# Interleaving plain and mixed products in a hand-ordered transformer-layer kernel, and moving an FFN weight sum, a v store and gate loads with it

## The chip, the cores and the metric

One core of one Trainium2 chip. The metric is device time in microseconds (us) of one launch, the median of the runs taken. The core has a matrix engine (PE), three elementwise engines (DVE, ACT, POOL), a sync engine (SP) that here issues most of the DMA transfers, and 16 DMA engines behind them. Each engine works through its own list of instructions in order; semaphores tie the lists together. A DMA that has to wait for something holds up whatever stands behind it on the engine that issues it.

## The reference, cut to what matters

One encoder layer on 1024 tokens of width 1024 (float32):

```python
h = rms_norm(x, g_norm1) * (1.0 + sc1) + sh1        # sc1, sh1, ... from c @ w_ada + b_ada
proj = h @ w_in                                     # 8 heads q,k,v + 12 heads q,k,v + two gates
qa, ka, va, qb, kb, vb, gates = split(proj)
o_a = neighbourhood_attention(rms_norm(qa), rms_norm(ka), va, rpb)
o_b = dilated_window_attention(rope(rms_norm(qb)), rope(rms_norm(kb)), vb)   # three dilations, merged
gate_a, gate_b = split(sigmoid(gates + b_gate))
x = x + gt1 * ((gate_a * (o_a @ w_proj_a) + gate_b * (o_b @ w_proj_b)) @ w_o)
h2 = rms_norm(x, g_norm2) * (1.0 + sc2) + sh2
a, up = split(h2 @ w_ffn_in)
x = x + gt2 * ((silu(a) * up) @ w_ffn_out)
```

The change touches how `h @ w_in` is formed for part of the heads, and when some of the weights of later stages are loaded and summed.

## The kernel before, in words

**Number format.** Every operand of a float32 matmul is split in a high and a low part, and each product is made of three passes (`PASS`: high by high, high by low, low by high). A weight tile `raw` is turned into `whi` by an ACT copy (L129) and into `wlo` by a subtraction (L132) on POOL or DVE. The tiles come from rings with a fixed number of buffers: `raw` 6, hi and lo 10 each, and 8 larger tiles named `big` (128 partitions by 1024). A load into a ring waits until the buffer's last reader is done.

**Units, steps and chunks.** The columns of `w_in` for q, k and v form ten units of two heads or so each; a unit is 384 columns wide (256 of q and k, 128 of v). Units 1 to 3 are computed plainly. Units 4 to 9 go in three pairs, (4,5), (6,7), (8,9), which the text calls pair 0, 1 and 2. A pair is computed with 7 products instead of 8, from sums of weights and sums of tokens (a Strassen-like scheme): `p1`, `p2`, `x1`, `x2`, `x4`, `x3`, `w22` in this order. A product is 4 tiles of 128 tokens (t0 to t3) by 4 chunks along the inner dimension; one chunk is three matmuls, L1183. So a pair is 112 chunks. The chunks of all units stand in one list, `stream`; the main loop runs over steps n = 6 to 91, and each takes the next 7 chunks (10 before step 28, 8 before step 10) and puts the attention work of earlier units between them. Pair 0 begins at chunk 192 (step 27), pair 1 at 304, pair 2 at 416; they end near step 75. Steps 76 to 91 compute the gates (`gate_pre`, matmul L832), again by sums of tokens and weights.

**What a product needs.** Products `p1`, `p2` and `x4` read plain tokens, which lie in SBUF (`hT`). Products `x1`, `x2`, `x3` and `w22` read mixed tokens (sums of tokens made earlier and kept in DRAM as `t_d`); SP loads them tile by tile, in a high and a low part (`sload`, L1169) into buffers of the hi and lo rings, named `smix`, every third one into a spare part of `hT`. When a product starts at chunk s, `sload` of tile t is issued at chunk s+4t-8, and the tile is needed at chunk s+4t. Its weights are loaded at s-27, -24, -21, -18 (L120, and L1140 for the tile `chain` of `x1`), mixed on POOL from s-17 on (L1145 to L1151) and split from s-14 on. `when(chunk, f)` hangs such work on a chunk.

**Where a product goes.** Each tile's result sits in one of two PSUM buffers `ps_d`, and the next but one tile waits for that buffer. `pair_evac` empties it: `p1` is copied to a sum A by ACT (L1116); `x1` makes B = A + p (L1118, DVE); `p2` finishes a tile of the pair's first unit out of A; `x2` adds to A and B (L1120, L1121); `x4`, `x3` and `w22` finish tiles out of B, B and A. A and B are slices of spare `hT` space. Finishing is `proj_post`: DVE adds the q and k part of the sum and PSUM into `qn` (L369); DVE adds the v part into a tile `vs` (L407), which ACT's DMA queue stores to `v_d` (L412); then come the norm (L372 to L387, ACT and DVE) and the rotation on POOL (L394 to L397). `vs` has two buffers, so the third add waits until the first store has landed.

**Other work in the same steps.** `w1_combos` (L900 to L917) forms sums of four tiles of a first FFN weight and keeps them in DRAM for later. It runs twice, in five parts on five consecutive steps: part 0 has SP load four tiles of 256 KB into two `big` buffers (L905), parts 1 to 4 are one POOL operation each (L909 to L915), and part 4 stores the four results. `W1MIX` sets the first step: 30 and 47. The adaLN modulation is computed along the way (weights `wa`, DVE multiply-adds L340, transposes L301). For the gates, `mixed_load` at step 76 loads 2 MB of mixed tokens (L777), and `gate_prep` by the table `GPREP` loads and splits gate weights: for the first pair of gates, part 0 at step 74 loads and splits the weights of the first two products, part 1 at step 77 loads the rest (L120 and L816), sums them (L820, L822 on POOL) and splits them.

**What sets the order.** PE's order is the order of the program, by hand. On the other engines a scheduler orders by priority and expected times, except for pinned work (most DMAs on SP, the POOL sums), which keeps program order.

Of the kernel before, what the change touches and what calls it, by code (L numbers as in the profile page):

```python
# [10 lines left out]
F32 = mybir.dt.float32  # L11
# [37 lines left out]
def hybrid_layer(ctx: ExitStack, tc: tile.TileContext, x, colp, wada1, wada2, bada2, wqkv, wg, wpa, wpb,  # L49
# [121 lines left out]
    ap_ = pool("attn", "right")  # L171
# [10 lines left out]
    yT = [ap_.tile([128, 4, S], F32, tag="qk", bufs=2, name="yT") for _ in range(2)]  # L182
    land = [big("land") for _ in range(NLAND)]
    for tag, n, bufs in (("bm", 512, 1), ("p", 512, 4), ("qn", 256, 9), ("rtab", 512, 1), ("acc2", 512, 1), ("pT", 512, 4),
                         ("stg", 512, 2), ("vs", 128, 2), ("ra", 64, 2), ("rb", 64, 2)):
        ap_.tile([128, n], F32, tag=tag, bufs=bufs, name="place")
    seq = [0]

# [45 lines left out]
            nc.vector.tensor_tensor_reduce(junk, xts[t], xts[t], 1.0, 0.0, ALU.mult, ALU.add, acc)  # L234

    def x_rstd(p):
        v, y, z = (ap_.tile([128, 2], F32, tag=f"xs{i}", bufs=2, name=f"xs{i}") for i in range(3))
        nc.scalar.activation(y, ss2[p], AF.Ln, scale=1.0 / D, bias=eps)
        nc.vector.tensor_scalar(v, ss2[p], 1.0 / D, EPS, op0=ALU.mult, op1=ALU.add)
        nc.scalar.activation(y, y, AF.Exp, scale=-0.5)  # L240
        nc.vector.tensor_mul(z, y, v)
        nc.vector.scalar_tensor_tensor(z, z, -0.5, y, op0=ALU.mult, op1=ALU.mult)
        nc.vector.scalar_tensor_tensor(y, z, 1.5, y, op0=ALU.add, op1=ALU.mult)
        xr[p] = y
# [115 lines left out]
        return deco  # L360

    @urgent(PP)
    def proj_post(U, t, pd=None, acc=None):
        pd = U.pd[t] if pd is None else pd
        qn = ap_.tile([128, 4, 64], F32, tag="qn", bufs=9, name="qn")
        U.qn[t] = qn
        pq = pd[:, :256].rearrange("p (h d) -> p h d", h=4)
        if acc is not None:
            nc.vector.tensor_add(qn, acc[:, :256].rearrange("p (h d) -> p h d", h=4), pq)  # L369
        vs = v_out(U, t, pd, acc)  # L370
        sq = ap_.tile([128, 256], F32, tag="sq", bufs=1, name="sq")
        nc.scalar.activation(sq, pd[:, :256] if acc is None else qn.rearrange("p h d -> p (h d)"), AF.Square)  # L372
        if acc is None:
            nc.scalar.activation(qn, pq, AF.Copy, scale=-1.0 / 128)
# [5 lines left out]
        nc.scalar.activation(y2, y, AF.Square)  # L380
        nc.vector.scalar_tensor_tensor(z, ss, 64 * EPS, y2, op0=ALU.add, op1=ALU.mult)
        nc.vector.scalar_tensor_tensor(r, z, -192.0, y, op0=ALU.add, op1=ALU.mult)
        rr = r[:, :, None].to_broadcast([128, 4, 64])
        if acc is None:
            nc.vector.tensor_tensor(qn, qn, rr, op=ALU.mult)
        else:
            nc.vector.scalar_tensor_tensor(qn, qn, -1.0 / 128, rr, op0=ALU.mult, op1=ALU.mult)  # L387
        if U.kind < 3:
            ra = ap_.tile([128, 4, 16], F32, tag="ra", bufs=2, name="ra")
            rb = ap_.tile([128, 4, 16], F32, tag="rb", bufs=2, name="rb")  # L390
            tb = U.tab[:, t]
            v4 = lambda z: z.rearrange("p (a b) c -> p a b c", a=2)
            tv = lambda f, c0, c1: tb[:, f, :, None, c0:c1].to_broadcast([128, 2, 2, c1 - c0])
            nc.gpsimd.tensor_tensor(v4(ra), v4(qn[:, :, 0:16]), tv(0, 0, 16), op=ALU.mult)  # L394
            nc.gpsimd.tensor_tensor(v4(rb[:, :, 0:8]), v4(qn[:, :, 8:16]), tv(1, 0, 8), op=ALU.mult)
            nc.gpsimd.tensor_tensor(v4(rb[:, :, 8:16]), v4(qn[:, :, 0:8]), tv(1, 8, 16), op=ALU.mult)
            nc.gpsimd.tensor_tensor(qn[:, :, 0:16], ra, rb, op=ALU.add)  # L397

    def v_out(U, t, pd, acc):
        if U.kind == 0:  # L400
            nc.scalar.activation(U.v[:, t, :], pd[:, 256:384], AF.Copy)
            return
        vs = ap_.tile([128, 128], F32, tag="vs", bufs=2, name="vs")
        if acc is None:
            nc.scalar.activation(vs, pd[:, 256:384], AF.Copy)
        else:
            nc.vector.tensor_add(vs, acc[:, 256:384], pd[:, 256:384])  # L407
# [382 lines left out]
    def gate_raw(i, q):  # L790
        return wload(wg[i, :, 4 * q:4 * q + 4, :], 512, True)
# [7 lines left out]

    def gate_prep(p, part):  # L800
        pr = GPAIRS[p]
        if part == 0:
            for i in pr if p == 0 else ():
                for q in (0, 1):
                    graw[i, q] = gate_raw(i, q)
            for nm, q in (("w11", 0), ("w12", 1)):
                for i in pr:
                    gwt[i, nm] = wsplit(graw[i, q])
            return
        if p == 0:  # L810
            z = big("wgx")
            for i in pr:
                for q in (2, 3):
                    graw[i, q] = gate_raw(i, q) if i == pr[0] else z[:, 512 * q - 1024:512 * q - 512]
            for q in (2, 3):
                pin(nc.sync.dma_start(graw[pr[1], q], wg[pr[1], :, 4 * q:4 * q + 4, :]))  # L816
        eng = nc.vector if p == 3 else nc.gpsimd
        for i in pr:
            r = [graw.pop((i, q)) for q in range(4)]
            eng.tensor_add(r[2], r[2], r[3])  # L820
# [102 lines left out]
    U = new_unit(0, w0)  # L923
# [141 lines left out]
    def when(p, f):  # L1065
        events.setdefault(p, []).append(f)

    def unit_of(u, w=None):
        if u == len(units):
            units.append(new_unit(u, w))  # L1070
        return units[u]
# [23 lines left out]
            for k in range(KT):  # L1095
                stream.append(lambda t=t, k=k: job(t, k))

    PROD = ("p1", "p2", "x1", "x2", "x4", "x3", "w22")
    SRC = {"p1": (0, 0), "p2": (0, 4), "x1": (1, 4), "x2": (0, 0), "x4": (0, 4), "x3": (1, 4), "w22": (1, 4)}
    sums, nmix = [], [0]  # L1100

    def pair_evac(nm, t, pd, ua, ub):
        if not sums:
            sums.extend(spare(q, 1536, F32) for q in range(2))
        A, B = (z[:, 384 * t:384 * t + 384] for z in sums)
        p = pd[:, :384]
        if nm == "p2":
            proj_post(unit_of(ua), t, pd, A)
        elif nm == "x4":
            proj_post(unit_of(ua), 4 + t, pd, B)  # L1110
        elif nm == "w22":
            proj_post(unit_of(ub), t, pd, A)
        else:
            with tc.high_priority(PP):
                if nm == "p1":
                    nc.scalar.activation(A, p, AF.Copy)  # L1116
                elif nm == "x1":
                    nc.vector.tensor_add(B, A, p)  # L1118
                elif nm == "x2":
                    nc.vector.tensor_add(A, A, p)  # L1120
                    nc.vector.tensor_add(B, B, p)  # L1121
                else:
                    nc.vector.tensor_add(A, A, p)
            if nm == "x3":
                proj_post(unit_of(ub), 4 + t, pd, B)

    def pair_units(ua):
        ub = ua + 1
        chain, ch = [], {}
        for nm in PROD:  # L1130
            s = len(stream)
            r, w = {}, {}
            e, k0 = SRC[nm]
            for k in range(4):
# [24 lines left out]
            for t in range(4):  # L1159
                sm = {}  # L1160
                if nm in TD:
# [7 lines left out]
                            pin(nc.sync.dma_start(fview(z).rearrange("p (k q) -> p k q", k=4), t_d[q, TD[nm], t]))  # L1169
# [790 lines left out]
```

## Time and profile before

| what | value |
|---|---|
| median of 3 runs | 1509.71 us (1507.7 to 1511.85) |
| profiled execution | 1507.33 us |
| its span, first to last instruction | 1505.5 us |
| granted PE clock, mean | 0.991 |
| PE busy | 1461.3 us, 97% of the span |
| PE weight load busy | 1240.9 us |
| DVE, ACT, POOL busy | 1096.3, 711.2, 732.5 us |
| DMA | 285.17 MB, 189 GB/s mean |

How to read it: a profile row gives the time of an instruction from the span's start, its duration, engine, source line and tiles ("out<-in"). In brackets stands how long the engine had been idle before it and what ended that idle time. A matmul's record is longer than the distance between two matmuls, because they are pipelined: a record of 128x384 reads some 0.33 us, and the next one starts some 0.16 us later.

### The profile page before, as it was taken

How to read it: one execution, taken by the hardware profiler on the slowest of the kernel's cores; microseconds unless marked ns; L12 is line 12 of the kernel's file. 1: busy time of each engine (PE TensorE's matmuls, PEld its weight loads, DVE VectorE, ACT ScalarE, POOL GpSimd, SP SyncE). 2: the span in 40 equal slices, each digit the busy share in tenths (PEclk: the TensorE clock that was granted, in tenths of full speed). 3: DMA queues.
4: the chain of work that ended last, by engine and by line, in shares of the span. 5: the costliest groups of instructions: out<-in, count | busy, mean ns of one | idle time of the engine just before them, and what ended most of it. 6: DMA issues, size and time to landing. Idle time of an engine off the chain costs nothing.

```text
span 1505.5 us, 24463 instructions
## 1 busy us (share of the span) xinstructions
PE 1461.3 (97%) x8024; PEld 1240.9 (82%) x8024; DVE 1096.3 (73%) x2144; ACT 711.2 (47%) x1807; POOL 732.5 (49%) x706
## 2 busy tenths in 40 slices
PE   8999998988999999999999999999999999999998
PEld 7999987888788777888888888888888888887886
DVE  6788856867877865576774597788767777599468
ACT  5666654654677865355432354233223333354442
POOL 0452357557354257247432301677767776104464
PEclk9999999999999999999999999999999999999999
DMA  9657769759855575693452225345443334898343
GB/s 355 235 176 238 206 196 305 229 177 297 260 178 175 175 242 198 229 351 99 130 203 96 90 89 181 126 130 179 151 129 107 110 106 145 277 374 281 98 151 102
DMA packets 189264, 285.17 MB, mean 189 GB/s; under 512 B 29488, under 2 KB 91600, under 8 KB 188368
## 3 DMA queue, kind: packets, MB, share of 16 engines
q1 hardware_dynamic: 170560, 269.96, 54.0%
q10 hardware_dynamic: 18576, 13.64, 2.8%
q8 instruction: 64, 1.05, 0.3%
q14 instruction: 64, 0.52, 0.1%
HBM read 218.67 MB, written 64.86 MB: 188 GB/s over the span
## 4 chain that ended last, share of the span: by engine, by line
PE 81%; DVE 7%; DMA 7%; ACT 2%; issue 2%; SPq 1%; POOL 0%; ACTq 0%; DVEq 0%; POOLq 0%
PE ps_v L1625 7%; PE ps_d L1625 7%; PE ps_s L1625 7%; PE ps_d L1183 7%; PE ps_t L1625 6%; PE ps_d L351 6%; PE ps_d L832 5%; PE ps_s L1795 3%; PE ps_d L1795 3%; PE ps_s L1560 2%; PE ps_d L1560 2%; PE ps_v L1795 2%; PE ps_t L1795 2%; PE ps_v L1560 1%; PE ps_v L832 1%
## 5 line engine op out<-in xcount | busy, mean ns | idle before, releaser
L129 ACT ACTIVATE whi<-raw 128x512 fp32r<-128x512 f32 (+2 forms) x313 | 182.0, 594 | 209.3 <-PE ps_s L1795 38.0
L132 POOL TENSOR_TENSOR wlo<-raw,whi 128x512 fp32r<-128x512 f32 (+2 forms) x142 | 178.9, 1268 | 176.7 <-ACT whi L129 161.1
L132 DVE TENSOR_TENSOR wlo<-raw,whi 128x512 fp32r<-128x512 f32 (+1 forms) x171 | 152.0, 906 | 55.2 <-ACT whi L129 50.0
L1183 PE MATMUL ps_d<-whi,hT 128*128 128x384 f32 x416 | 120.1, 353 | 17.1 <-DVE vs L407 5.3
L351 PE MATMUL ps_d<-whi,hT 128*128 128x384 f32 x384 | 101.2, 338 | 0.0
L1575 POOL TENSOR_TENSOR e<-e,c 128x512 f32<-128x512 f32 x44 | 68.8, 1565 | 61.1 <-DVE c L1705 37.0
L1183 PEld LDWEIGHTS ps_d<-whi,hT 128*128 128x128 f32 x416 | 78.9, 195 | 20.9 <-issue 7.1
L129 ACT ACTIVATE whi<-ws 128x512 fp32r<-128x512 f32 x60 | 37.7, 628 | 119.4 <-DVE ws L1642 76.8
L832 PE MATMUL ps_d<-hT,whi 128*128 128x512 f32 x256 | 81.8, 401 | 0.1
L1183 PE MATMUL ps_d<-whi,smix 128*128 128x384 f32 x256 | 73.8, 348 | 7.7 <-DMA smix<-t_d 5.1
L132 POOL TENSOR_TENSOR wlo<-m,whi 128x512 fp32r<-128x512 f32 x35 | 51.3, 1476 | 55.0 <-ACT whi L129 55.0
L1573 ACT ACTIVATE e<-e 128x512 f32<-128x512 f32 x44 | 27.5, 631 | 93.8 <-DVE e L1708 64.7
L1183 PE MATMUL ps_d<-wlo,hT 128*128 128x384 f32 x208 | 71.7, 345 | 0.0
L351 PEld LDWEIGHTS ps_d<-whi,hT 128*128 128x128 f32 x384 | 69.6, 188 | 0.6 <-issue 0.6
L132 POOL TENSOR_TENSOR wlo<-chain,whi 128x384 fp32r<-128x384 f32 x36 | 38.0, 1057 | 55.4 <-ACT whi L129 53.6
L351 PE MATMUL ps_d<-wlo,hT 128*128 128x384 f32 x192 | 64.2, 334 | 0.0
L619 ACT ACTIVATE P<-P,st 128x256 f32<-128x256 f32 (+2 forms) x100 | 45.7, 458 | 28.8 <-DVE st L617 28.5
L1625 PE MATMUL ps_v<-h2T,whi 128*128 128x512 f32 x192 | 59.2, 389 | 0.0
L1625 PE MATMUL ps_s<-h2T,whi 128*128 128x512 f32 x192 | 59.1, 389 | 0.0
L340 DVE SCALAR_TENSOR_TENSOR acc<-wa,cact,acc 128x512 f32<-128x512 f32 x56 | 50.2, 897 | 10.7 <-DMA wa<-in_wada_dram 10.5
L1625 PE MATMUL ps_d<-h2T,whi 128*128 128x512 f32 x184 | 56.7, 390 | 0.0
L1574 DVE TENSOR_TENSOR e<-e 128x512 f32<-128x512 f32 x44 | 43.7, 1000 | 17.2 <-ACT e L1573 17.0
(447 smaller groups left out, 4498.6 us busy)
## 6 DMA issues: line engine op xcount, KB each, us to landing
raw<-in_w_dram SPq DMA_DIRECT2D x139, 256.0 KB, 3.1
raw<-in_wqkv_dram SPq DMA_DIRECT2D x116, 192.0 KB, 4.2
ga_d<-e SPq DMA_DIRECT2D x77, 256.0 KB, 2.0
raw<-ga_d SPq DMA_DIRECT2D x77, 256.0 KB, 2.7
wa<-in_wada_dram SPq DMA_DIRECT2D x32, 512.0 KB, 5.4
smix<-t_d SPq DMA_DIRECT2D x64, 256.0 KB, 3.0
m<-in_w_dram SPq DMA_DIRECT2D x44, 256.0 KB, 5.3
hT<-t_d SPq DMA_DIRECT2D x40, 256.0 KB, 5.1
```

Of the source, the lines that this page charges most:

```text
L129: h = nc.scalar.activation(hi[:, :n], r, AF.Copy)
L132: (eng or nc.gpsimd).tensor_sub(lo[:, :n], r, fview(hi[:, :n]))
L340: nc.vector.scalar_tensor_tensor(ada_acc[c], wa, cact[:, kk:kk + 1], ada_acc[c], op0=ALU.mult, op1=ALU.add)
L351: nc.tensor.matmul(pd[:, :384], tok(a, k, t), U.w[k][b][:, :384], start=(k == 0 and i == 0), stop=(k == KT - 1 and i == 2))
L619: nc.scalar.activation(C.P[h][:nq, c], C.P[h][:nq, c], AF.Exp, scale=-1.0, bias=nm, accum_out=sm)
L832: nc.tensor.matmul(pb, w[x][:, k * 128:(k + 1) * 128], b[y][k], start=(k == 0 and q == 0), stop=(k == 3 and q == 2))
L1183: nc.tensor.matmul(pd[:, :384], lhs, w[k][b][:, :384], start=(k == 0 and i == 0), stop=(k == 3 and i == 2))
L1560: nc.tensor.matmul(pbs[hf], h2T[a][:, k, t * 128:(t + 1) * 128], wow[hf, k][b], start=(n == 0 and (a, b) == PASS[0]), stop=(n == KT - 1 an ...
L1574: nc.vector.tensor_mul(sg, sg, a)
L1575: nc.gpsimd.tensor_mul(sg, sg, up)
L1625: nc.tensor.matmul(pb, w[p][:, k * 128:(k + 1) * 128], b[q][:, k], start=(k == 0 and i == 0), stop=(k == 3 and i == 2))
L1795: nc.tensor.matmul(pb[m], o[0][a][:, m * 128:(m + 1) * 128], o[1][b], start=(k == 0 and i == 0), stop=(k == HT - 1 and i == 2))
```

## The change

1. **Order of products.** In each pair the order is now `p1`, `x1`, `p2`, `x2`, `x4`, `x3`, `w22`: plain and mixed tokens alternate at the start of the pair. The weights and tokens of `x1` are thereby needed 16 chunks earlier, those of `p2` 16 later.
2. **FFN weight sums.** `W1MIX` is (69, 74) instead of (30, 47).
3. **Token loads.** For `x1`, `x2` and `x3` the tiles t0, t1, t2 are issued at s-15+3t instead of s+4t-8: 7, 8 and 9 chunks earlier. t3 and all of `w22` stay.
4. **v.** `vs` gets three buffers. In the products of the pair's second unit (`x3`, `w22`) the v part is not summed into `vs` but in place into the sum tile (B or A), and the store to `v_d` reads that.
5. **Gate loads.** For the first pair of gates the loads of part 0 are at step 73 (split at 74 as before), those of part 1 at step 75 (sums and splits at 77 as before).
6. The splits of the very first product (`p1` of pair 0) are no longer pinned.
7. Small tiles: `x_rstd` shares buffers of the tags rv, ry, rz, and a filler `AFILL` shrinks from 384 to 64, which makes room for the third `vs`.

From about line 800 on, lines of the changed kernel lie three higher: L1183 becomes L1186, L905 becomes L908.

```diff
-GPREP = {74: (0, 0), 77: (0, 1), 82: (1, 0), ...}
-W1MIX = (30, 47)
+GPREP = {73: (0, -2), 74: (0, 0), 75: (0, -1), 77: (0, 1), 82: (1, 0), ...}
+W1MIX = (69, 74)
...
-                         ("stg", 512, 2), ("vs", 128, 2), ("ra", 64, 2), ("rb", 64, 2)):
+                         ("stg", 512, 2), ("vs", 128, 3), ("ra", 64, 2), ("rb", 64, 2)):
...
-    def v_out(U, t, pd, acc):
+    def v_out(U, t, pd, acc, here):
...
-        vs = ap_.tile([128, 128], F32, tag="vs", bufs=2, name="vs")
+        vs = acc[:, 256:384] if here else ap_.tile([128, 128], F32, tag="vs", bufs=3, name="vs")
...
     def gate_prep(p, part):
         pr = GPAIRS[p]
-        if part == 0:
-            for i in pr if p == 0 else ():
+        if part == -2:
+            for i in pr:
                 for q in (0, 1):
                     graw[i, q] = gate_raw(i, q)
+            return
+        if part == 0:
             for nm, q in (("w11", 0), ("w12", 1)):
                 for i in pr:
                     gwt[i, nm] = wsplit(graw[i, q])
             return
-        if p == 0:
+        if part == -1:
             z = big("wgx")
...
+            return
         eng = nc.vector if p == 3 else nc.gpsimd
...
-    PROD = ("p1", "p2", "x1", "x2", "x4", "x3", "w22")
+    PROD = ("p1", "x1", "p2", "x2", "x4", "x3", "w22")
...
         elif nm == "w22":
-            proj_post(unit_of(ub), t, pd, A)
+            proj_post(unit_of(ub), t, pd, A, True)
...
             if nm == "x3":
-                proj_post(unit_of(ub), 4 + t, pd, B)
+                proj_post(unit_of(ub), 4 + t, pd, B, True)
...
-                    w[k] = wsplit(ch[k] if nm in ("x1", "x2", "x3") else r[k], None, True)
+                    w[k] = wsplit(ch[k] if nm in ("x1", "x2", "x3") else r[k], None, s > 192)
...
-                    when(s + 4 * t - 8, sload)
+                    when(s - 15 + 3 * t if nm in ("x1", "x2", "x3") and t < 3 else s + 4 * t - 8, sload)
```

How the change moves instructions stands in the prediction, at the places it speaks of; there the rows name an engine's instructions in program order, by line and tile.

More of the change, by code (lines that the diff above doesn't have):

```diff
@@ L30 @@
 GPHASE = ("w11", "w12", "x1", "x4")
-GPREP = {74: (0, 0), 77: (0, 1), 82: (1, 0), 84: (1, 1), 86: (2, 0), 88: (2, 1), 90: (3, 0)}
+GPREP = {73: (0, -2), 74: (0, 0), 75: (0, -1), 77: (0, 1), 82: (1, 0), 84: (1, 1), 86: (2, 0), 88: (2, 1), 90: (3, 0)}
 GLOAD = {81: 1, 85: 2, 89: 3}
-W1MIX = (30, 47)
+W1MIX = (69, 74)
 MC11 = {0: (5, 6, 7, 2), 1: (0, 1)}
@@ L39 @@
 PP, QT, AQ, AT, AV = 100, 0, 0, 0, 0
-EDGE, CFILL, AFILL, OFILL = 480, 64, 384, 32
+EDGE, CFILL, AFILL, OFILL = 480, 64, 64, 32
 WARM = 40
@@ L236, in x_rstd @@
     def x_rstd(p):
-        v, y, z = (ap_.tile([128, 2], F32, tag=f"xs{i}", bufs=2, name=f"xs{i}") for i in range(3))
+        v, y, z = (ap_.tile([128, 2], F32, tag=i, bufs=3, name="xs") for i in ("rv", "ry", "rz"))
         nc.scalar.activation(y, ss2[p], AF.Ln, scale=1.0 / D, bias=eps)
@@ L362, in proj_post @@
     @urgent(PP)
-    def proj_post(U, t, pd=None, acc=None):
+    def proj_post(U, t, pd=None, acc=None, here=False):
         pd = U.pd[t] if pd is None else pd
@@ L369, in proj_post @@
             nc.vector.tensor_add(qn, acc[:, :256].rearrange("p (h d) -> p h d", h=4), pq)
-        vs = v_out(U, t, pd, acc)
+        v_out(U, t, pd, acc, here)
         sq = ap_.tile([128, 256], F32, tag="sq", bufs=1, name="sq")
```

## The prediction

> **What bounds the kernel now.** I read the page first: PE is busy nearly all of the span, and the chain that ended last lies on PE for the most part, with DVE and DMA behind it.
>
> ```profile
> PE 1461.3 (97%) x8024; PEld 1240.9 (82%) x8024; DVE 1096.3 (73%) x2144; ACT 711.2 (47%) x1807; POOL 732.5 (49%) x706
> PE 81%; DVE 7%; DMA 7%; ACT 2%; issue 2%; SPq 1%; POOL 0%; ACTq 0%; DVEq 0%; POOLq 0%
> ```
>
> The change removes no matmul, so it can only fill idle time of PE. The second view is a table by stretches (columns: stretch, its length, busy time of PE, PE weight load, DVE, ACT and POOL, granted clock, DMA share, GB/s).
>
> ```profile
> 560.00:1350.00 790.00, 790.00 (x3628) 652.32 (x3627) 568.80 (x778) 302.40 (x562) 400.60 (x282) 1.00 0.49 166
> 240.00:250.00 10.00, 9.71 (x68) 8.94 (x69) 7.76 (x18) 4.75 (x15) 9.54 (x9) 0.83 1.07 396
> 300.00:310.00 10.00, 4.91 (x36) 4.23 (x37) 9.40 (x26) 4.45 (x19) 5.88 (x11) 0.75 0.76 245
> 310.00:320.00 10.00, 10.00 (x62) 9.42 (x60) 2.73 (x11) 6.30 (x21) 7.87 (x14) 0.91 0.70 227
> 350.00:360.00 10.00, 6.55 (x35) 5.58 (x36) 7.48 (x8) 2.10 (x4) 10.00 (x9) 0.83 1.08 374
> 420.00:430.00 10.00, 7.71 (x57) 6.72 (x56) 7.34 (x25) 7.44 (x25) 3.93 (x5) 1.00 0.47 142
> 440.00:470.00 30.00, 30.00 (x226) 26.79 (x225) 20.33 (x64) 20.14 (x63) 17.55 (x18) 1.00 0.72 230
> 530.00:540.00 10.00, 7.75 (x45) 5.50 (x44) 4.97 (x14) 5.59 (x16) 7.46 (x6) 0.86 0.61 223
> ```
>
> From 560 to 1350 us PE never idles. The idle time that can be had lies in the pairs and the first gates, 200 to 540 us. There the clock falls after a long gap: 0.75 in the stretch of the longest one. So a gap costs its length and, behind it, (1 - clock) times the stretch. The third view is PE's timeline around its large gaps (start, duration, what; in brackets the gap and what ended it).
>
> ```profile
> 205.13 0.44 PE L1183 MATMUL ps_d<-whi,hT 128*128 128x384 f32 x1 [2.79 <-ACT qn L374]
> 233.12 0.41 PE L1183 MATMUL ps_d<-whi,smix 128*128 128x384 f32 x1 [1.53 <-DVE hT L1118]
> 234.67 0.62 PE L1183 MATMUL ps_d<-whi,smix 128*128 128x384 f32 x2 [0.96 <-DMA smix<-t_d]
> 240.29 0.66 PE L1183 MATMUL ps_d<-whi,hT 128*128 128x384 f32 x1 [3.61 <-DMA hT<-t_d]
> 295.48 0.41 PE L1183 MATMUL ps_d<-whi,hT 128*128 128x384 f32 x1 [1.68 <-DMA hT<-t_d]
> 305.25 0.66 PE L1183 MATMUL ps_d<-whi,hT 128*128 128x384 f32 x1 [5.09 <-DVE vs L407]
> 354.81 0.41 PE L1183 MATMUL ps_d<-whi,smix 128*128 128x384 f32 x1 [3.45 <-DMA smix<-t_d]
> 386.45 0.43 PE L301 MATMUL ps_t<-acc,ones 128*32 128x128 f32 x8 [2.15 <-ACT PT L641]
> 399.75 0.41 PE L1183 MATMUL ps_d<-whi,smix 128*128 128x384 f32 x1 [1.08 <-DVE vs L407]
> 425.30 0.44 PE L1183 MATMUL ps_d<-whi,hT 128*128 128x384 f32 x1 [2.29 <-ACT hT L1116]
> 535.50 0.50 PE L832 MATMUL ps_d<-hT,wlo 128*128 128x512 f32 x1 [2.17 <-POOL wlo L132]
> ```
>
> These eleven gaps add to 26.8 us. I take them one by one: is the wait that ended last still there after the change?
>
> **The change part by part.**
>
> *FFN weight sums away from steps 30 and 47, tokens of x1 earlier (term 1).* The gaps at 233 to 240 us are in x1 of pair 0, t1 and t2. SP's timeline shows why its tokens were late, and the table of waits of SP what held it:
>
> ```profile
> 214.08 13.31 SPq L905 DMA_DIRECT2D w1m<-in_w_dram x4
> 227.49 0.38 SPq L120 DMA_DIRECT2D raw<-in_wqkv_dram x1
> 227.97 3.63 SPq L1169 DMA_DIRECT2D smix<-t_d x2
> ...
> SPq L905 <- DMA v_d<-vs: 16.6, 3, 6.8
> SPq L1169 <- PE ps_d L1183: 43.6, 24, 5.6
> ```
>
> The four loads of w1m held SP for 13.31 us, and the tokens queued behind. In program order, SP at this place reads before (x1's t0 is row 100, t1 row 104):
>
> ```order
> 98 L1140 DMA chain<-in_wqkv_dram 128x384
> 99 L120 DMA raw<-in_wqkv_dram 128x384 x2
> 100 L1169 DMA smix<-t_d 128x512 x2
> 101 L120 DMA raw<-in_wqkv_dram 128x384
> 102 L905 DMA w1m<-in_w_dram 128x512 x4
> 103 L120 DMA raw<-in_wqkv_dram 128x384
> 104 L1169 DMA smix<-t_d 128x512 x2
> ```
>
> and now, for the same tiles of x1 (t0 row 97, t1 row 102, t2 row 104):
>
> ```order
> 97 L1172 DMA smix<-t_d 128x512 x2
> 98 L325 DMA brow<-in_bada_dram 128x1x128
> 99 L315 DMA wa_3176<-in_wada_dram 128x1024
> 100 L315 DMA wa_3317<-in_wada_dram 128x1024
> 101 L315 DMA wa_3466<-in_wada_dram 128x1024
> 102 L1172 DMA smix<-t_d 128x512 x2
> 103 L120 DMA raw<-in_wqkv_dram 128x384
> 104 L1172 DMA hT<-t_d 128x512 x2
> ```
>
> The w1m loads are gone from between the tokens; adaLN weights stand there instead. The row of the pair's matmuls gives the time of a chunk:
>
> ```profile
> L1183 PE MATMUL ps_d<-whi,hT x416: 333/334/660, 200.1 to 508.7; 128*128 128x384 f32 x139
> ```
>
> 308.6 us over 336 chunks of the three pairs is 0.92 us. t1 and t2 are now issued 16 and 17 chunks, about 15 us, before use, where it was 8 chunks, 7.3 us. Gone: 1.53 + 0.96 + 3.61 = 6.10, and (1 - 0.83) x 10 = 1.7 of clock behind them: **-7.8**.
>
> *Token of x2 in pair 1 (term 2).* The gap of 3.45 at 354.81 waited for a token that is now asked for 8 chunks, 7.4 us, earlier: more than it was late. With 1.7 of clock (350 to 360): **-5.1**.
>
> *v in place (term 3).* The longest gap, 5.09, is the first tile of pair 1, which waits for the PSUM buffer of pair 0's last product. DVE's and ACT's timelines before it:
>
> ```profile
> 298.24 0.41 DVE L369 TENSOR_TENSOR qn<-hT,ps_d 128x256 f32<-128x256 f32 x1
> 300.11 0.16 DVE L381 SCALAR_TENSOR_TENSOR rz<-ss,ry 128x4 f32<-128x4 f32 x1 [1.46 <-ACT ry L380]
> 301.73 1.55 DVE L340 SCALAR_TENSOR_TENSOR acc<-wa,cact,acc 128x512 f32<-128x512 f32 x1
> 304.82 0.28 DVE L407 TENSOR_TENSOR vs<-hT,ps_d 128x128 f32<-128x128 f32 x1
> 299.87 0.21 ACT L380 ACTIVATE ry<-rv 128x4 f32<-128x4 f32 x1 [1.91 <-DMA u_d<-stg]
> ```
>
> L369 has read its part of the buffer at 298.65; L407, which frees it, starts at 304.82. With two vs tiles the scheduler had put seven instructions between, among them L381, which waits for an ACT instruction behind a store's issue. The DVE program from L369 of this tile (t2 of w22) to its L407, before:
>
> ```order
> 585 L369 TENSOR_TENSOR qn<-hT,ps_d 128x256
> 586 L381 SCALAR_TENSOR_TENSOR rz<-ss_4518,ry 128x4
> 587 L340 SCALAR_TENSOR_TENSOR acc_4330<-wa_4554,cact,acc_4330 128x512
> 588 L382 SCALAR_TENSOR_TENSOR rz<-rz,rv 128x4
> 589 L340 SCALAR_TENSOR_TENSOR acc_4330<-wa_4554,cact,acc_4330 128x512
> 590 L387 SCALAR_TENSOR_TENSOR qn<-qn,rz 128x256
> 591 L376 TENSOR_REDUCE ss_4620<-sq 128x4
> 592 L381 SCALAR_TENSOR_TENSOR rz<-ss_4574,ry 128x4
> 593 L407 TENSOR_TENSOR vs<-hT,ps_d 128x128
> ```
>
> and now, from t1's L369 to t2's L407:
>
> ```order
> 578 L369 TENSOR_TENSOR qn<-hT,ps_d 128x256
> 579 L407 TENSOR_TENSOR hT<-hT,ps_d 128x128
> 580 L376 TENSOR_REDUCE ss_4556<-sq 128x4
> 581 L381 SCALAR_TENSOR_TENSOR rz<-ss_4499,ry 128x4
> 582 L382 SCALAR_TENSOR_TENSOR rz<-rz,rv 128x4
> 583 L369 TENSOR_TENSOR qn<-hT,ps_d 128x256
> 584 L407 TENSOR_TENSOR hT<-hT,ps_d 128x128
> ```
>
> L407 follows L369 directly and waits for no store. The buffer is free some 6 us sooner, so all 5.09 go. Behind it the clock costs (1 - 0.75) x 10 + (1 - 0.91) x 10 = 3.4, less 0.1 that falls into the gap: **-8.4**. The gap at 399.75, also L407: **-1.1**.
>
> *Gate loads (term 4).* The gap at 535.50 waits for a low part that POOL made late, since the weights came late. SP's and POOL's timelines:
>
> ```profile
> 518.48 5.84 SPq L777 DMA_DIRECT2D hT<-t_d x8
> 525.14 0.92 SPq L120 DMA_DIRECT2D raw<-in_wg_dram x2
> 530.58 1.29 POOL L820 TENSOR_TENSOR raw<-raw 128x512 f32<-128x512 f32 x1 [20.52 <-DMA raw<-in_wg_dram]
> ```
>
> The weights stood behind 2 MB of mixed tokens. In SP's program they now stand ahead of them (before):
>
> ```order
> 246 L867 DMA sig_d<-ga 128x512
> 247 L777 DMA hT<-t_d 128x4x128 x8
> 248 L867 DMA sig_d<-ga 128x512
> 249 L120 DMA raw<-in_wg_dram 128x512 x2
> 250 L816 DMA wgx<-in_wg_dram 128x512 x2
> ```
>
> and now:
>
> ```order
> 247 L920 DMA w_d<-w1m 128x512 x4
> 248 L120 DMA raw<-in_wg_dram 128x512 x4
> 249 L908 DMA w1m<-in_w_dram 128x512 x4
> 250 L120 DMA raw<-in_wg_dram 128x512 x2
> 251 L818 DMA wgx<-in_wg_dram 128x512 x2
> 252 L870 DMA sig_d<-ga 128x512
> 253 L777 DMA hT<-t_d 128x4x128 x8
> ```
>
> The loads pass 9 transfers, the first of which waited for the gate result. POOL had been idle for 20.52 us, so its sums start as soon as the loads land, at the latest the 6.66 us earlier that lie between 518.48 and 525.14. Gone: 2.17, and (1 - 0.86) x 10 = 1.4 of clock: **-3.6**. Here a rule bears on it: the Trainium skill (TensorE: Matmul & The Clock Gate, "What's actually happening") says that the clock halves after about 3.4 us of idle time, in windows that run free. By that rule alone this gap of 2.17 would cost no clock and the forecast would be 1.4 us higher. The trace shows it both ways: 0.86 behind 2.17 here, 1.00 behind 2.29 in the stretch from 420; I go by the trace.
>
> *What stays.* The gaps at 205.13 (ACT late), 295.48 (w22 keeps its load step), 386.45 and 425.30 (ACT in order) have no cause that the change removes: 0, between -8.9 (their sum, should the new order dissolve them) and 0.
>
> *What is added.* The w1m loads, sums and stores now fall at steps 69 to 78, about 470 to 520 us. One POOL sum, and the room there:
>
> ```profile
> L909 POOL TENSOR_TENSOR w1m<-w1m x2: 1260/1272/1283, 236.5 to 346.9; 128x512 f32<-128x512 f32 x2
> 480.00:500.00 20.00, 20.00 (x152) 18.10 (x151) 18.37 (x66) 17.13 (x61) 4.28 (x4) 1.00 0.65 198
> 510.00:520.00 10.00, 8.63 (x60) 5.77 (x59) 7.81 (x33) 8.70 (x30) 0.06 (x1) 1.00 0.19 51
> ```
>
> Four sums of 1.27 us, 5.1 a set, meet a POOL that is busy for 4.28 of 20 and 0.06 of 10 us; DMA is at 0.19 in the second stretch. I take 0. If the loads block SP for 13.31 us again, the last w22's tokens lose their cover of 8 chunks, 7.3 us: 13.31 - 7.3 = 6 us at most.
>
> x1 needs its weights 16 chunks earlier in pair 0, right at the start of the pair. A sum there and a split take about 1 us each on POOL:
>
> ```profile
> L1145 POOL TENSOR_TENSOR chain<-chain,raw x12: 1000/1008/1021, 211.7 to 429.2; 128x384 f32<-128x384 f32 x12
> ```
>
> Four of each are 8 us, within the 14.7 us of the product p1, but not much ahead of it. If each of four inner chunks comes one such operation late, that is 4 us; if none, 0. I take 2. Last, reshuffled work on ACT and DVE can meet PE anew: between 0 and one gap of the size of 425.30 a pair, 6.9; I take one, 2.3.
>
> Sum: -7.8 - 5.1 - 8.4 - 1.1 - 3.6 + 2 + 2.3 = -21.7. The profiled execution took 1507.33, so 1485.6; it lies 2.4 below the median of 1509.71, and on that footing the forecast is **1488**. Its own range: -26 with half of the four others gone (-4.5) gives 1479; with costs of 4 and 6.9, 1494.6.
>
> **The rivals.** 0.3%, about what a measurement can tell here, is 4.5 us.
>
> *Tokens stay late, 0.2.* SP's waits for buffers that PE frees are 43.6 us in 24 waits before; a load that is issued earlier only waits longer if its buffer's reader sets the time. Then term 2 and half of term 1 stay: -21.7 + 5.1 + 3.9 = -12.7, **1497**. For it: that row. Against it: the waits that ended the gaps are transfers behind other transfers, and 3.45 is less than what is gained.
>
> *Earlier tokens block SP, slower, 0.07.* The loads of x1, x2 and x3 stand 7 to 9 chunks earlier on SP, ahead of weight loads. If they wait for buffers there, the weights behind them come late. Weights have 13 chunks, 12 us, from load to split; the longest wait for a buffer was 5.6, so two such in a row, with a slow landing, decide it. At the price of term 2, 5.1 a product, nine products cost 46: 1488 + 46 = **1534**; from six products on it is slower. The Trainium skill (DMA: Bandwidth & Descriptors, "Anatomy of one DMA") says that a semaphore wait is served by the issuing sequencer before dispatch, so whatever is behind waits too. The 13.31 us of SP above agree.
>
> *Other waits take over, 0.1.* If pairs are bound by DVE and ACT throughout, and not by single waits, what is freed is lost at the next buffer: **1507**, within 0.3%. For it: DVE is busy for 9.40 of 10 us before the longest gap. Against it: from 440 to 470 the same products ran with PE at 30.00 of 30 and DVE at 20.33.
>
> **How the numbers follow.** Forecast 0.6, rivals 0.2, 0.07 and 0.1, 0.03 for the rest. Faster: 0.6 + 0.2 and a part of the rest, 0.82; same 0.1; slower 0.08. The range runs from 1478 (under the forecast's low end) over the first rival with its costs at the upper bounds, 1497 + 6.6 = 1504; it leaves out 0.2.
>
> **What would show it.** Right: no gap over 1 us that ends on L407, or on a token of x1 or x2; the stretch around 305 us of the pair boundary at clock 1.00; the first gate products after pair 2 without a gap; gaps left at the first p1 and around adaLN's transposes. Wrong: SP's w1m loads holding it for over 7 us near 470 or 505; POOL's wlo ending PE's gaps in x1 of pair 0; SP's waits for PE's buffers well over 43.6 with weight splits late.

## The result and the profile after

| | before | changed |
|---|---|---|
| median | 1508.7 us (4 runs, 1504.68 to 1511.85) | 1494.12 us (4 runs, 1493.69 to 1495.56) |
| profiled execution, its span | 1507.33, 1505.5 us | 1495.56, 1493.8 us |

The ratio is 0.9906, with a 95% interval of 0.9881 to 0.9932: faster by 0.9%, some 14 us. The forecast was a gain of 21.7 us, with a range that holds the measured time.

The page of the changed kernel: the work is the same, PE is busy 3 us less, and the span is 11.7 shorter.

```profile
PE 1458.3 (98%) x8024; PEld 1237.0 (83%) x8024; DVE 1102.1 (74%) x2144; ACT 711.0 (48%) x1807; POOL 732.3 (49%) x706
```

From 200 to 560 us the kernel before had 14 gaps of PE of 0.5 us and more, 28.7 us in all; the changed kernel has 20, 22.7 us in all. Nine of the 20, from PE's timeline (start, duration, what; in brackets the gap and what ended it):

```profile
204.26 0.45 PE L1186 MATMUL ps_d<-whi,hT 128*128 128x384 f32 x1 [1.48 <-ACT qn L374]
239.93 0.41 PE L1186 MATMUL ps_d<-whi,smix 128*128 128x384 f32 x1 [1.42 <-DVE vs L407]
302.72 0.45 PE L1186 MATMUL ps_d<-whi,hT 128*128 128x384 f32 x1 [2.39 <-ACT hT L1119]
351.95 0.44 PE L1186 MATMUL ps_d<-whi,hT 128*128 128x384 f32 x1 [1.86 <-DVE hT L1124]
383.10 0.41 PE L1186 MATMUL ps_d<-whi,smix 128*128 128x384 f32 x1 [1.16 <-DVE rz L382]
384.47 0.64 PE L1186 MATMUL ps_d<-whi,smix 128*128 128x384 f32 x2 [0.78 <-DMA smix<-t_d]
498.73 0.73 PE L835 MATMUL ps_d<-hT,whi 128*128 128x512 f32 x2 [0.97 <-ACT whi L129]
500.08 0.50 PE L835 MATMUL ps_d<-hT,wlo 128*128 128x512 f32 x1 [0.63 <-POOL wlo L132]
503.57 0.70 PE L581 MATMUL ps_v<-PT,v 128*64 128x128 f32 x4 [0.91 <-ACT PT L572]
```

None of the gaps of 3.4 to 5.1 us is left; the longest is 2.39. But PE's waits from 200 to 560 us (what for: us in total, times, longest) show how many smaller ones took their place:

```profile
PE ps_d L1186 <- ACT hT L1119: 3.5, 3, 2.4
PE ps_d L1186 <- DVE hT L1124: 2.8, 2, 1.9
PE ps_d L1186 <- DVE vs L407: 2.3, 2, 1.4
PE ps_v L438 <- DVE tot L705: 1.7, 1, 1.7
PE ps_d L1186 <- DMA smix<-t_d: 0.8, 1, 0.8
```

Tokens (smix) are down to 0.8 us. What ends most of the waits now is DVE and ACT; the first three rows, 8.6 us, are instructions that empty PSUM. The stretches, with the granted clock third from the end:

```profile
300.00:310.00 10.00, 7.61 (x53) 6.97 (x54) 3.16 (x10) 4.71 (x15) 7.54 (x12) 0.83 0.87 305
380.00:390.00 10.00, 8.06 (x40) 6.79 (x39) 7.24 (x24) 5.60 (x22) 2.99 (x3) 0.83 1.02 263
500.00:510.00 10.00, 9.01 (x40) 6.66 (x40) 7.93 (x22) 9.05 (x29) 9.67 (x9) 0.66 0.54 167
550.00:1340.00 790.00, 790.00 (x3628) 652.51 (x3627) 569.35 (x777) 301.18 (x560) 400.76 (x281) 1.00 0.49 166
```

By (1 - clock) times the stretch, an estimate that also counts idle time within a stretch, the clock costs 1.7 + 1.7 + 3.4 = 6.8 us there. In the kernel before it cost 1.7 + 3.4 + 1.7 + 1.4 = 8.2 in the stretches shown with the prediction, and 3.2 in two more:

```profile
200.00:210.00 10.00, 7.21 (x33) 6.89 (x32) 4.50 (x18) 7.04 (x24) 4.28 (x10) 0.83 0.74 227
380.00:390.00 10.00, 7.85 (x57) 7.01 (x56) 7.97 (x24) 6.10 (x19) 3.44 (x3) 0.85 0.78 236
```

So by this estimate 11.4 - 6.8 = 4.6 of the 11.7 us of span are clock. The pages of the two profiles give less: PE's busy time, for the same 8024 matmuls, fell by 3.0 us, and the other 8.7 us are idle time. The stretch without gaps behind (550 to 1340) is as long as before.

### The profile page after: what moved, and what is told of

The parts are those of the page before. It is cut to its first block, busy times and chain, and to the rows that moved or that the text cites. A ratio compares the mean times of both kernels' runs of the same rounds, so it can differ in the third digit from the quotient of the medians.

```text
span 1493.8 us, 24484 instructions
## 1 busy us (share of the span) xinstructions
PE 1458.3 (98%) x8024; PEld 1237.0 (83%) x8024; DVE 1102.1 (74%) x2144; ACT 711.0 (48%) x1807; POOL 732.3 (49%) x706
## 4 chain that ended last, share of the span: by engine, by line
PE 61%; DVE 4%; issue 1%; DMA 1%; ACT 1%; POOL 0%; SPq 0%; ACTq 0%; DVEq 0%; POOLq 0%
PE ps_v L1628 7%; PE ps_d L1628 7%; PE ps_s L1628 7%; PE ps_t L1628 6%; PE ps_d L835 6%; PE ps_s L1798 3%; PE ps_d L1798 2%; PE ps_d L1563 2%; PE ps_s L1563 2%; PE ps_t L1798 2%; PE ps_v L1798 2%; DVE wlo L132 1%; PE ps_v L1563 1%; PE ps_v L835 1%; PE ps_v L1414 1%; PE ps_t L1414 1%
## 5 line engine op out<-in xcount | busy, mean ns | idle before, releaser
L1186 PE MATMUL ps_d<-whi,hT 128*128 128x384 f32 x416 | 118.3, 347 | 9.8 <-DVE hT L1124 2.8
L1186 PEld LDWEIGHTS ps_d<-whi,hT 128*128 128x128 f32 x416 | 77.0, 190 | 14.6 <-PE ps_d L1186 4.4
L1186 PE MATMUL ps_d<-whi,smix 128*128 128x384 f32 x256 | 73.8, 346 | 6.5 <-DVE vs L407 1.4
L1186 PE MATMUL ps_d<-wlo,hT 128*128 128x384 f32 x208 | 70.6, 339 | 1.0 <-POOL wlo L132 1.0
L132 POOL TENSOR_TENSOR wlo<-gl,whi 128x512 fp32r<-128x512 f32 x30 | 40.1, 1352 | 34.3 <-ACT whi L129 34.3
L394 POOL TENSOR_TENSOR ra<-qn,rtab 128x64 f32<-128x64 f32 x48 | 21.0, 437 | 71.3 <-DVE qn L385 50.0
```

Source lines behind the costliest of these rows:

```text
L132: (eng or nc.gpsimd).tensor_sub(lo[:, :n], r, fview(hi[:, :n]))
L1186: nc.tensor.matmul(pd[:, :384], lhs, w[k][b][:, :384], start=(k == 0 and i == 0), stop=(k == 3 and i == 2))
```

## The experiments

All times are set against the kernel before on the same chip; "loss" is a kernel's ratio less the changed kernel's 0.9906, times 1509 us, and each ratio is known to about 0.2%, 3 us. My theory was that each part of the change removes its own gaps (terms). The rivals: the parts stand in for each other or need each other; or freed time is lost at the next wait.

Where a kernel gains or loses is seen by the first matmul of each pair and of the gates, counted off in the traces (336 records of L1183 or L1186 a pair). The times are us from the span's start, from one profiled execution of each kernel; executions of one kernel differ by some us.

| first matmul of | before | changed | u_w1 | u_sload | u_order | u_gate | u_v2 |
|---|---|---|---|---|---|---|---|
| pair 0 | 200.1 | 200.5 | 200.7 | 199.5 | 199.9 | 200.5 | 200.3 |
| pair 1 | 305.3 | 292.3 | 298.3 | 297.1 | 296.9 | 292.9 | 296.7 |
| pair 2 | 405.7 | 390.8 | 405.6 | 399.9 | 402.9 | 389.5 | 394.1 |
| gates | 508.9 | 498.7 | 508.7 | 508.7 | 511.3 | 500.3 | 500.1 |
| end of the span | 1505.5 | 1493.8 | 1500.1 | 1503.9 | 1506.0 | 1506.8 | 1494.8 |

The changed kernel gains 14.9 us up to the start of pair 2, and loses 4.7 of them again between there and the first gate product.

### FFN weight sums put back: u_w1

```diff
-W1MIX = (69, 74)
+W1MIX = (30, 47)
```

> The changed kernel with the FFN weight sums back at steps 30 and 47. Theory of terms (each part of the change removes its own gaps): the 7.8 us of the gaps in x1 of pair 0 come back, so about 6 to 8 us slower than the changed kernel's 1494.1. Theory of cover (the early token loads alone already hide SP's block of 13.31 us, and the sums cost something at their new place, where the gate products now wait 0.97 + 0.63 + 0.91 us and the clock is 0.66 from 500 to 510 us): at most 2 us slower, or up to 4 us faster, and the stretch 500 to 510 back at clock 1.00.

Measured: 0.9946 (0.9925 to 0.9967), a loss of 6.0 us. That is near the size of the term, but not its mechanism. No wait of x1 in pair 0 came back. The 6 us are also a balance: by the table u_w1 is 14.8 us behind the changed kernel at the start of pair 2, and only 6.3 at the end. From 500 to 510 us its clock is 1.00, and its first gate products do not wait, as the theory of cover had it for this stretch; so the sums cost something at their new place. In pair 0 PE waits at x4 for a low part, and POOL's timeline shows why:

```profile
258.68 0.69 PE L1186 MATMUL ps_d<-wlo,hT 128*128 128x384 f32 x1 [2.35 <-POOL wlo L132]
255.46 1.27 POOL L918 TENSOR_TENSOR w1m<-w1m 128x512 f32<-128x512 f32 x1
256.69 0.98 POOL L1152 TENSOR_TENSOR raw<-raw,chain 128x384 f32<-128x384 f32 x1
257.64 1.94 POOL L132 TENSOR_TENSOR wlo<-raw,whi 128x384 fp32r<-128x384 f32 x2
214.07 3.50 SPq L908 DMA_DIRECT2D w1m<-in_w_dram x4
```

A sum of the FFN weights (L918, 1.27 us) stands on POOL between x4's own sums and splits. This wait is one of several that are longer than in the changed kernel (2.87 at the first tile of x2 in pair 0 for 1.42, 2.69 at the first tile of x4 in pair 1 for 0.92); what makes the others longer was not traced. On SP the four loads now hold the queue for 3.50 us where it was 13.31 in the kernel before, with the tokens already ahead of them.

### Token loads put back: u_sload

```diff
-when(s - 15 + 3 * t if nm in ("x1", "x2", "x3") and t < 3 else s + 4 * t - 8, sload)
+when(s + 4 * t - 8, sload)
```

> The changed kernel with the token loads of x1, x2, x3 back at s+4t-8. Theory of terms: term 2, the token of x2 in pair 1, comes back, 5.1 us, and perhaps part of x1's gaps: 5 to 8 us slower than 1494.1. Theory of cover (without the w1m loads in the way the old lead of 8 chunks is enough): within 2 us of 1494.1, no gap over 1 us that ends on a token.

Measured: 0.9971 (0.9954 to 0.9987), a loss of 9.8 us, more than either theory said, and again for the most part not through tokens: PE's waits on them are 4.4 us from 200 to 560, where they are 0.8 in the changed kernel, and 2.08 of them are in w22, whose loads are the same in both. The largest gap is at the first tile of x2 in pair 1. PE's and DVE's timelines:

```profile
345.25 0.66 PE L1186 MATMUL ps_d<-whi,hT 128*128 128x384 f32 x1 [5.45 <-ACT sq L372]
335.70 1.50 DVE L340 SCALAR_TENSOR_TENSOR acc<-wa,cact,acc 128x512 f32<-128x512 f32 x1 [1.37 <-DMA wa<-in_wada_dram]
337.45 1.18 DVE L340 SCALAR_TENSOR_TENSOR acc<-wa,cact,acc 128x512 f32<-128x512 f32 x1
339.45 0.74 DVE L340 SCALAR_TENSOR_TENSOR acc<-wa,cact,acc 128x512 f32<-128x512 f32 x1
340.98 1.56 DVE L340 SCALAR_TENSOR_TENSOR acc<-wa,cact,acc 128x512 f32<-128x512 f32 x1
344.32 0.41 DVE L369 TENSOR_TENSOR qn<-hT,ps_d 128x256 f32<-128x256 f32 x1
```

What empties the PSUM buffer of p2 (L369, and L407 behind it at 344.72) stands on DVE behind four adaLN operations, the first of which waited for its weights `wa`. The profile names ACT as what ended PE's wait, but L407 on DVE is what frees the buffer. In the changed kernel the L369 of the same tile (t2 of p2) runs ten us sooner, ahead of the adaLN operations, 0.3 us after the tile's last matmul where it is 6.6 in u_sload:

```profile
334.04 0.41 DVE L369 TENSOR_TENSOR qn<-hT,ps_d 128x256 f32<-128x256 f32 x1
342.56 2.44 DVE L340 SCALAR_TENSOR_TENSOR acc<-wa,cact,acc 128x512 f32<-128x512 f32 x2
```

Loads of `wa` and tokens share SP; with the tokens moved, the adaLN work stands elsewhere relative to p2. How the scheduler came to this order no run shows.

### Both put back: u_w1_sload

> Both of the above undone. Theory of terms: 7.8 + 5.1 = 13 us slower, so about 1507, with gaps that end on tokens of x1 or x2. Theory of cover: each part alone hid the same gaps, so only both together bring them back: more than the sum of the two single kernels' losses. Rival (other waits take over): less than 5 us slower.

Measured: 1.0041 (1.0026 to 1.0057), slower than the kernel before, a loss of 20.4 us where the single losses add to 15.8. The excess of 4.6 us is on the side of the theory of cover, but within the joint uncertainty of four ratios (some 6 us), so it is not shown that the parts stand in for each other. The gaps that came back are not those on tokens of x1 that the theory meant: PE's largest are 6.84 and 4.59, at the first tile of x2 in pairs 1 and 0, where p2's sums on DVE come late. What is left of the change, the new order above all, is a loss without these two parts.

### The order alone, and all but the order: b_order, u_order

In b_order only the line of `PROD` differs from the kernel before; in u_order only that line differs from the changed kernel.

> The changed kernel with the products back in the order p1, p2, x1, x2, x4, x3, w22; all else as changed. Theory of terms as predicted (the order itself carries no term, it only adds 2 to 4.3 us of reshuffled work): 0 to 4 us faster than the changed kernel's 1494.1. Rival (the alternation is what spreads DVE's and ACT's evacuation work, so the order carries part of the gain): 4 to 10 us slower. With the old order and the old loads, the two kernels with loads and sums undone showed 1515 in the new order where the kernel before needs 1509.7: that speaks for the first.

> The kernel before with the new order of products alone. If the order by itself spreads the emptying of the PSUM buffers (theory of spread), it gains 4 to 10 us over the kernel before. If the order pays only with its tokens asked for early and SP free (theory of cover: x1 comes 16 chunks earlier, and in pair 0 it meets the w1m loads that hold SP for 13.31 us), it is 0 to 8 us slower than the kernel before. The kernel with the sums and the token loads undone, at 1.0041 of the kernel before, speaks for the second.

Measured: u_order 1.0004 (0.9988 to 1.002), a loss of 14.8 us: without the order the rest of the change gains nothing. b_order 1.0064 (1.0045 to 1.0083): the order alone costs 9.7 us. My expectation for u_order, that the order carries no term, was wrong, and so was the theory of spread for b_order, that it gains by itself. The theory of cover had the direction, with 0 to 8 us; but the w1m loads that it blamed held SP for 1.81 us there, not for 13.31. Both gaps of 5 to 7 us in b_order are at the first tile of x2, in pair 0 and in pair 1; PE's, DVE's and SP's timelines:

```profile
242.63 0.66 PE L1183 MATMUL ps_d<-whi,smix 128*128 128x384 f32 x1 [5.12 <-ACT sq L372]
352.50 0.66 PE L1183 MATMUL ps_d<-whi,hT 128*128 128x384 f32 x1 [6.87 <-DMA mod_d<-brow]
342.67 1.33 DVE L340 SCALAR_TENSOR_TENSOR acc<-wa,cact,acc 128x512 f32<-128x512 f32 x1 [2.51 <-DMA wa<-in_wada_dram]
350.87 0.40 DVE L369 TENSOR_TENSOR qn<-hT,ps_d 128x256 f32<-128x256 f32 x1
339.33 6.44 SPq L315 DMA_DIRECT2D wa<-in_wada_dram x2
345.86 1.41 SPq L1169 DMA_DIRECT2D smix<-t_d x3
```

It is the same picture as in u_sload: adaLN weights come late on SP (6.44 us for two issues), DVE waits for them ahead of p2's L369, and PE for DVE; the tokens stand behind them too. In u_order, what PE waits for most are the copies and sums that empty PSUM:

```profile
205.95 0.44 PE L1186 MATMUL ps_d<-whi,hT 128*128 128x384 f32 x1 [3.79 <-ACT qn L374]
308.59 0.54 PE L1186 MATMUL ps_d<-whi,hT 128*128 128x384 f32 x1 [3.66 <-ACT hT L1119]
349.26 0.41 PE L1186 MATMUL ps_d<-whi,smix 128*128 128x384 f32 x1 [2.94 <-DVE hT L1124]
423.29 0.44 PE L1186 MATMUL ps_d<-whi,hT 128*128 128x384 f32 x1 [2.63 <-ACT hT L1119]
```

The old order finishes units in products 2, 5, 6, 7 of a pair, so that from x4 of one pair to p2 of the next four of five products carry the norms and stores; the new one puts two light products (p1, x1) behind the three heavy ones. That this spreading is what the order gives is argued from the list, not shown by a run.

### v: u_v and u_v2

u_v passes no `True` to `proj_post`, so v always goes into `vs`, with three buffers; u_v2 has two buffers besides.

> The changed kernel with v always summed into vs, which keeps its three buffers. Theory of terms with in-place v as the cause: the gap at the start of pair 1 that ends on L407 comes back, 5 to 9 us slower than 1494.1. Rival: the third buffer alone is enough, since a third store can be under way: within 2 us of 1494.1, and no gap over 1.5 us that ends on L407.

> The changed kernel with v always summed into vs and vs back at two buffers: all of the change to v undone. With three buffers and no sum in place it took 0.9886 of the kernel before, no worse than the changed kernel. Theory of terms (third buffer or sum in place, either cures the gap of 5.09 and its clock): 7 to 10 us slower than 1494.1, with a gap over 2 us at the start of pair 1 or 2 that ends on L407. Rival (the gap was an accident of the old order of work, not of vs): within 3 us of 1494.1.

Measured: u_v 0.9886 (0.9862 to 0.991), u_v2 0.9905 (0.9886 to 0.9923). The whole change to v is worth nothing that can be measured, though it does what it says. u_v has no gap at the first tile of pair 1, so the third buffer alone is enough for that; its longest wait on L407 is 2.28, at the first tile of x2 in pair 0, where the changed kernel waits 1.42. PE's timeline and the stretches of u_v2:

```profile
296.73 0.66 PE L1186 MATMUL ps_d<-whi,hT 128*128 128x384 f32 x1 [4.82 <-DVE vs L407]
290.00:300.00 10.00, 5.18 (x33) 4.40 (x31) 7.53 (x19) 4.20 (x17) 5.80 (x10) 0.73 0.88 293
300.00:310.00 10.00, 10.00 (x70) 9.77 (x69) 5.00 (x19) 7.09 (x23) 8.89 (x17) 0.93 0.91 320
```

The gap of 5.09 at the start of pair 1 is back as 4.82, with its clock. But the changed kernel, rid of it, stands for 2.39 at the third tile of p1 (302.72) and pays the clock there (0.83 in 300 to 310); u_v2 has no such gap, since ACT catches up while PE waits. By the table u_v2 is 4.4 us behind at the start of pair 1; at the first matmul of x1 it is 2.4 behind (314.9 against 312.6), and at the end 1.0. So about half of the freed time is lost at the next wait, and most of the rest later, within what a measurement tells.

### Gate loads: u_gate, u_w1_gate, i_gate72

In u_gate the gate loads are issued in the steps of their splits again, 74 and 77; u_w1_gate has the FFN sums back at 30 and 47 besides; in i_gate72 the first loads come at step 72 instead of 73.

> The changed kernel with the gate loads back in the steps of their splits (74 and 77). Theory of terms: the gap of 2.17 us at the third and fourth gate product and its clock come back, and the first gate products wait longer than the 0.97 us they wait now, since their loads then stand behind the four w1m loads of step 74 too (5.43 us on SP): 4 to 9 us slower than 1494.1. Rival (the loads are hidden anyway): within 1.5 us.

> The changed kernel with both the FFN weight sums and the gate loads as before. Undoing the gate loads alone cost all 14 us of the gain, undoing the sums alone 6. Theory of company (the sums at steps 69 and 74 sit on SP and POOL in front of the gates, and the early gate loads are what pays for that): with both undone it loses less than with the gate loads alone undone, 1500 to 1506, that is 6 for the sums and at most 3.6 for the gates. Theory of terms (independent parts): 6 + 14, so about 1514.

> The changed kernel with the first gate loads at step 72 instead of 73, ahead of the four w1 stores of step 73, which held SP from 487.60 to 491.39. If those stores make the first gate weights late (PE waits 0.97, 0.63 and 0.91 us at 498 to 504 us, and the clock is 0.66 from 500 to 510): up to 2 us of gaps and 3.4 us of clock go, so 1489 to 1492. Rival (the waits move on to ACT and POOL, which make four splits in a row there): within 1 us of 1494.1.

Measured: u_gate 1.0005 (0.999 to 1.0019), a loss of 14.9; u_w1_gate 0.9945 (0.9927 to 0.9963), which is u_w1's 0.9946, as the theory of company had it; i_gate72 0.9911 (0.9895 to 0.9927), no difference. The first gate weights are earlier in i_gate72, but a gap of 2.56 us stands in w22 now:

```profile
488.25 0.66 PE L1186 MATMUL ps_d<-whi,smix 128*128 128x384 f32 x1 [2.56 <-issue]
```

With the FFN sums at their old place the early gate loads are worth nothing; with the sums in front of the gates they are worth the whole gain. By the table u_gate keeps up with the changed kernel to the first gate product (1.6 us behind) and loses 13.0 by the end. Its first gate product, and a chain behind it, from the timelines of PE, SP, POOL and DVE:

```profile
500.26 0.73 PE L835 MATMUL ps_d<-hT,whi 128*128 128x512 f32 x2 [2.92 <-ACT whi L129]
516.96 0.93 SPq L120 DMA_DIRECT2D raw<-in_wg_dram x2
522.38 1.29 POOL L823 TENSOR_TENSOR raw<-raw 128x512 f32<-128x512 f32 x1 [12.69 <-DMA raw<-in_wg_dram]
537.86 1.27 POOL L918 TENSOR_TENSOR w1m<-w1m 128x512 f32<-128x512 f32 x1
539.15 0.32 SPq L920 DMA_DIRECT2D w_d<-w1m x1
539.53 0.93 SPq L718 DMA_DIRECT2D ut<-u_d x2
542.97 0.69 DVE L747 TENSOR_TENSOR oacc<-ut,ps_t 128x512 f32<-128x512 f32 x1 [6.74 <-DMA ut<-u_d]
543.81 0.45 PE L566 MATMUL ps_t<-ident,P 128*128 128x128 f32 x1 [4.84 <-DVE oacc L747]
```

The first gate weights stand on SP behind four loads of w1m (1.96 us from 490.89), and their product waits 2.92 us, as expected. The second ones come late too, POOL makes the gate sums late, the last FFN sum (L918) stands behind them on POOL, its store (L920) waits for it on SP, and the load of `ut`, which attention needs, stands behind the store. The chain ends in 4.84 of the 14.8 us that PE stands from 490 to 560 in gaps over 0.3 us; in the changed kernel these are 3.9 us. Of the others, 1.98 and 0.62 end on POOL's low parts, and 2.64 on an operation of DVE (L730) that was not traced further. The changed kernel has the same rows 13 us earlier:

```profile
526.39 0.38 SPq L920 DMA_DIRECT2D w_d<-w1m x1
526.82 1.07 SPq L718 DMA_DIRECT2D ut<-u_d x2
```

### What is left at the start of pair 1: i_p1dve, i_all

i_p1dve copies p1 into A on DVE (`nc.vector.tensor_copy(A, p)`) instead of ACT. i_all joins this with u_v and i_gate72.

> The changed kernel with the sum A of p1 copied by DVE instead of ACT. If what is left at the start of pair 1 (2.39 us and clock 0.83 from 300 to 310) and of pair 2 (0.86) is set by ACT's order, where the copy stands behind nine exponentials, 2 to 5 us faster than 1494.1. Rival (DVE, busy for 74% of the span, is as late as ACT was): within 2 us of 1494.1, and gaps at the same places that end on the DVE copy.

> The changed kernel with three small changes that were each no worse alone: v always into vs with three buffers, the sum A of p1 copied by DVE, and the first gate loads at step 72. If their small gains (ratios to the kernel before of 0.9886, 0.9892 and 0.9911 where the changed kernel has 0.9906) are real and add up, 3 to 5 us faster than 1494.1; if they were chance or stand in for each other, within 2 us.

Measured: i_p1dve 0.9892 (0.9872 to 0.9912), i_all 0.9897 (0.9877 to 0.9917): both about 2 us or less below the changed kernel, the rival's side. DVE is as late as ACT was at the same place:

```profile
302.30 0.45 PE L1186 MATMUL ps_d<-whi,hT 128*128 128x384 f32 x1 [2.96 <-DVE hT L1119]
```

No version tried beats the changed kernel by more than its interval.

## Why the prediction was right, and where its steps were not

The direction was right and the size two thirds of the forecast: the six large waits that I crossed out are gone. The seventh, at the third tile of w22 in pair 1 (1.08 us), is still there, as 1.16 and 0.78. The account of what each part is worth was not right, and that the total still fell into the range is in part luck: terms that were worth nothing, and parts that were worth more than booked, made up for each other.

- **FFN sums (term 1, -7.8).** Their move is worth 6.0 in the finished kernel, but as a balance: 14.8 us up to the start of pair 2, less 8.5 from there to the end, where I took 0. I had put it down to SP and the tokens; with the early tokens no wait of x1 is left for it, and the wait that was traced is POOL's, where a sum of 1.27 us stood between x4's splits.
- **Token of x2 (term 2, -5.1).** The token's wait went. Undoing the early loads costs 9.8, and the largest wait that comes with it (5.45) is one for DVE: SP's order also sets when adaLN's weights come, and the operations on them stand on DVE ahead of what empties PSUM. My step "asked for 8 chunks earlier" looked at one queue and one tile.
- **v (terms of -8.4 and -1.1).** The step that failed outright, in size. "So all 5.09 go" was true, and worth 0 by u_v2. I had taken one wait as the only one; the next, ACT's copy of p1, was 2.4 us behind and drew the clock down as well. The rival "other waits take over" is right for this stretch and wrong for the whole.
- **Gate loads (term 4, -3.6).** Alone worth 0 (u_w1 against u_w1_gate). They pay for the FFN sums at their new place: without them, 14.9 us go. I had set the cost of that place at 0 with a bound of 6 and named POOL's and DMA's idle shares as cover. The shares were read rightly, but they say nothing of the order, and there the cost lay: in loads behind loads, and in a store waiting on SP for a late POOL sum. The rule of the Trainium skill (DMA: Bandwidth & Descriptors, "Anatomy of one DMA") that a wait is served at the issuing sequencer tells this, and the row of 539.15 with `ut` behind it agrees; I had applied it to tokens only.
- **The order (no term).** Worth 14.8 in company and -9.7 alone. I had priced it only as a risk.
- **What stays (0) and what is added (+4.3).** The four waits that I left standing, 8.9 us, came down to 3.0 at the same tiles, and I had booked none of that. Against it, 17.8 us of gaps of 0.5 us and more stand at places where the kernel before had 1.9; I had taken 2.3 for reshuffled work and 2 for x1's weights. This is where the missing 7 us are.
- **The clock.** That gaps cost clock too was right: 3.0 to 4.6 of the 11.7 us, where I had booked 8.1. The rule of the Trainium skill (TensorE: Matmul & The Clock Gate, "What's actually happening") of about 3.4 us of idle time does not fit the changed kernel: 0.66 from 500 to 510, behind gaps of 0.97, 0.63 and 0.91. The measurement decides.
- **The signs.** Tokens of x1 and x2 kept theirs: no gap over 1 us ends on one. Three signs of being right did not come: a gap of 1.42 still ends on L407, at the first tile of x2 in pair 0; behind the start of pair 1 (292.3) the clock is 0.83 from 300 to 310; and the first gate products wait 0.97 and 0.63. Of the signs of being wrong, SP's waits for PE's buffers rose from 43.6 to 51.8 us; the w1m loads held SP for 6.24 and 5.43 us at their new place, under the 7 that I had named.

The losses on undoing one part add to 6.0 + 9.8 + 0 + 14.8 + 14.9 = 45.5 us, of a gain of 14: each of four parts is needed for the whole of it, the gate loads only with the sums at their new place, and no share of the gain belongs to one of them. Open stays how much of the order's worth is the spreading of the finishing work, since no run changed that alone.

## What to carry to other kernels

Price a moved transfer or sum by everything that stands behind it on its queue, including work that has nothing to do with it: here adaLN weights and a store of FFN sums decided much of it, not only the tokens and gates that were meant. When a large gap is removed, look for the wait that comes next in the same stretch before its whole length, and its clock, is booked. Parts of a reordering should be tested by undoing each from the finished kernel as well as by adding each alone: the order of products cost 9.7 us alone and was worth 14.8 with the rest.

## What the runs showed of the hardware that was not expected

The granted clock fell without any single long gap: to 0.66 over 10 us behind three gaps that add to 2.5 us, while a gap of 2.29 in the kernel before left it at 1.00. Small DVE operations on SBUF data took very uneven times; L382 works on 128x4 elements (shortest, median, longest in ns):

```profile
L382 DVE SCALAR_TENSOR_TENSOR rz<-rz,rv x80: 144/164/1253, 62.8 to 511.9; 128x4 f32<-128x4 f32 x80
```

In the changed kernel its median is 161 ns where POOL is idle (50 of them) and 316 where POOL works for over half of it (29), and L387's 420 and 804; for L369, which reads PSUM, it is 412 and 410. So some of the DVE work that stands ahead of the emptying of PSUM takes about twice as long beside POOL's work. That POOL is the cause is not shown, since no run changed its work alone.
